# One power on GpSimd for the root, a VectorE-only residual update in a fixed order, and earlier places for the statistics' matmuls

## The chip, the cores and the metric

The kernel runs on one core of a Trainium2 chip. The metric is the device time of one execution in microseconds (us); lower is better. TensorE (PE) multiplies, VectorE (DVE) and GpSimd (POOL) do elementwise work, ScalarE (ACT) does activations and copies, and SyncE (SP) issues the loads.

## What is computed

A stack of eight sublayers works on 512 tokens of width 1024 in float32: two layers of a mixer with four gated branches and a SiLU feed-forward, then a recurrent block, an MLP, banded attention and another MLP. Around every sublayer stands an RMS norm; the four sublayers of the first block also norm their output before they add it to the residual:

```
def rmsnorm(x, g):
    y = xf * lax.rsqrt(jnp.mean(xf * xf, axis=-1, keepdims=True) + EPS)
    return (y * g.astype(jnp.float32)).astype(x.dtype)
...
    x = x + rmsnorm(merged @ w_out[l], g_post_mix[l])
    h = rmsnorm(x, g_pre_ffn[l])
    f = (jax.nn.silu(h @ w_ffn_gate[l]) * (h @ w_ffn_up[l])) @ w_ffn_down[l]
    x = x + rmsnorm(f, g_post_ffn[l])
```

## The kernel before, in words

Activations lie transposed: eight tiles of 128 features by 512 tokens. `self.x[k]` (tile name `xf`) is the residual. Each operand of a product is split into a high part and a low part (`xh`, `xl`; `wh`, `wl`), and `mm3` adds three matmuls: high by high, high by low, low by high. So a product needs the high part first (line 147) and the low part from its second or third matmul on (lines 148 and 149). The split of the residual for the next product (`norm_split`, by way of `split`) is an ACT copy with the gain as its scale (line 108) and a DVE subtraction (line 109).

The norm's factor never multiplies the operand: it is one number for each token and is applied to the result of the next product. It is made in four steps: squares are summed into `S` tile by tile (lines 215 to 219), `stats` lets PE sum them over the features (line 199, one column for each 128 tokens, result `ps_t`), `rsqrt` takes the root (lines 183 to 190: twelve small DVE instructions, a first guess from the bits and three Newton steps), and `spread` transposes the factor back over all partitions on PE (line 208). An ACT copy brings it to SBUF as `rb`.

`closing` ends the two mixers and the two feed-forwards (four times in all). It makes the last product of the sublayer in eight output tiles; the last four are made in two halves of 256 tokens, H0 and H1. After H0's four tiles come H0's statistics, root, transposes and `rb` while PE works on H1's tiles; `update` then multiplies each output tile by `rb` (line 248, DVE), adds it to the residual (line 249, POOL) and splits the new residual for the next sublayer's first product `self.first`, three output tiles at once, which begins with H0 as well. H1 gets the same one half later.

A scheduler sets the order of the instructions on each engine from data dependences and a timing model of its own. Inside `tc.issue_after(ins)` an instruction is placed after `ins`; `behind` in `gemm` uses this to hold the steps `k >= a` of a product back until the named instruction has its place in PE's queue. The lines that the change touches in `closing`:

```
behind = [(0, self.summed if j else None), (0, self.turned if j == 3 else None)] if cs is H1 else []
...
self.first = self.gemm(first, n.xs, gnext[2] if len(gnext) > 2 else "wide", halves=True,
                       behind=[(2, self.summed), (5, self.turned)])
```

`summed` is the last statistics matmul, `turned` the last transpose, `j` counts the four tiles made in halves.

Of the kernel before, what the change touches and what calls it, by code (L numbers as in the profile page):

```python
# [9 lines left out]
F32 = mybir.dt.float32  # L10
F32R = mybir.dt.float32r
I32 = mybir.dt.int32
AF = mybir.ActivationFunctionType
ALU = mybir.AluOpType
# [3 lines left out]
P = 128  # L18
# [3 lines left out]
EPS = 1e-6  # L22
# [4 lines left out]
ALL, H0, H1, ALLP = slice(0, 512), slice(0, 256), slice(256, 512), slice(0, P)  # L27
# [38 lines left out]
class Net:  # L66
    def __init__(self, ctx, tc, d, out):
        self.tc, self.nc, self.d, self.out = tc, tc.nc, d, out
        self.small = ctx.enter_context(tc.tile_pool(name="small", bufs=1))
        self.base = ctx.enter_context(tc.tile_pool(name="base", bufs=1))  # L70
        self.psum = ctx.enter_context(tc.tile_pool(name="psum", bufs=1, space=PSUM))
        self.prm = self.small.tile([P, NPRM], F32, name="prm")
        self.tab = self.small.tile([P, NTAB], F32, name="tab")
        self.uid = 0
        self.wide = 0
        self.after = []
# [99 lines left out]

    def rsqrt(self, y, src, n, scale):

        nc = self.nc
        v = self.t(self.small, "rs_v", 2, (P, 16))[:, :n]  # L180
        m = self.t(self.small, "rs_m", 2, (P, 16))[:, :n]
        w = self.t(self.small, "rs_w", 2, (P, 16))[:, :n]
        nc.vector.tensor_scalar(out=v, in0=src, scalar1=scale, scalar2=EPS, op0=ALU.mult, op1=ALU.add)
        nc.vector.tensor_scalar(out=m, in0=src, scalar1=-0.5 * scale, scalar2=-0.5 * EPS, op0=ALU.mult, op1=ALU.add)
        nc.vector.tensor_scalar(out=y.bitcast(I32), in0=v.bitcast(I32), scalar1=-0.5,
                                scalar2=float(0x5F3759DF), op0=ALU.mult, op1=ALU.add)
        for _ in range(3):
            nc.vector.tensor_tensor(out=w, in0=y, in1=y, op=ALU.mult)
            nc.vector.tensor_tensor(out=w, in0=w, in1=m, op=ALU.mult)
            self.rooted = nc.vector.scalar_tensor_tensor(out=y, in0=w, scalar=1.5, in1=y, op0=ALU.add, op1=ALU.mult)  # L190

    def stats(self, r, S, n, cs):

# [32 lines left out]
        n.rb = self.t(self.base, "rb", 2)  # L226
        return n

    def norm_split(self, n, k, cs):
        if n.xs[k] is None:  # L230
            n.xs[k] = self.pair(self.base, "x", KT)
        h, l = n.xs[k]
        x = self.x[k][:, cs]
        return self.split((h[:, cs], l[:, cs]), x, n.g[:, k:k + 1] if n.g is not None else None)

    def norm_step(self, n, k, cs):
        self.norm_split(n, k, cs)
# [4 lines left out]

    def update(self, fs, rb, n, cs):

        nc = self.nc
        for k in range(KT):
            f, x = fs[k][:, cs], self.x[k][:, cs]
            nc.vector.tensor_tensor(out=f, in0=f, in1=rb, op=ALU.mult)  # L248
            nc.gpsimd.tensor_tensor(out=x, in0=x, in1=f, op=ALU.add)
            last = self.norm_split(n, k, cs)  # L250
        return last


    def scores(self, it, qb):
# [91 lines left out]
    def mix(self, l, gnext):  # L346
        nc, tc, d = self.nc, self.tc, self.d
        V, S_, G = nc.vector, nc.scalar, nc.gpsimd
        N = self.norm
        xs, r, rb = N.xs, N.r, N.rb  # L350
# [6 lines left out]
        with tc.tile_pool(name=f"att{l}", bufs=1, reuse_waits="tile") as ap:  # L357
# [17 lines left out]
            for c in range(2):  # L375
                wh, wl = chunk(4 + c)
                for k in range(4):
                    x = xs[c * 4 + k]
# [6 lines left out]
            ps = self.ps("t")  # L385
# [29 lines left out]
            for i in range(4):  # L415
                f = vv[i // 2][:, i % 2 * 256:i % 2 * 256 + 256]
# [150 lines left out]
        with tc.tile_pool(name=f"gate{l}", bufs=1, reuse_waits="tile") as gp:  # L567
            self.wide = 0
            early = [self.gemm([chunk(16 + n)], xs)[0] for n in range(4)]
            br = {}  # L570
            for nm, fs in (("c", [outs["c0"], outs["c1"]]), ("b", [outs["b0"], outs["b1"]]),
                           ("d", [outs["d0"], outs["d1"]]), ("a", aout)):
                br[nm] = []
                for j, f in enumerate(fs):
                    if j % 2 == 0:
                        both = self.pair(gp, "wf", 5, (P, 2, T))
                    hl = (both[0][:, j % 2], both[1][:, j % 2])
                    self.split(hl, f)
                    br[nm].append(hl)
            ms = []  # L580
            for i in range(KT):
                m = self.t(gp, "m", 2)
                wo = None
                for n, nm in enumerate("cbda"):
                    ps = early.pop(0) if early else self.gemm([chunk(16 + i * 4 + n)], xs)[0]
                    g = self.t(gp, "g", 2)
                    V.tensor_tensor(out=g, in0=ps, in1=rb, op=ALU.mult)
                    S_.activation(out=g, in_=g, func=AF.Tanh, scale=0.5)
                    if nm == "a":
                        w = self.load(d["w_br"][l, i, :, 768:], 512)  # L590
                    else:
                        wo = wo or self.load(d["w_br"][l, i, :, :768], 768)
                        w = (wo[0][:, n * 256:n * 256 + 256], wo[1][:, n * 256:n * 256 + 256])
                    ps = self.gemm([w], br[nm])[0]
                    if n == 0:
                        V.scalar_tensor_tensor(out=m, in0=g, scalar=1.0, in1=ps, op0=ALU.add, op1=ALU.mult)
                    else:
                        V.scalar_tensor_tensor(out=g, in0=g, scalar=1.0, in1=ps, op0=ALU.add, op1=ALU.mult)  # L598
                        G.tensor_tensor(out=m, in0=m, in1=g, op=ALU.add)  # L599
                hl = self.pair(gp, "m_", 8)  # L600
                self.split(hl, m, scale=0.5)
                ms.append(hl)
            fs = [self.t(mp, tag, 4 if tag == "aout" else 1) for tag in ["aout"] * 4 + ["b0", "b1", "c0", "c1"]]

            def evac(S, i, ps, cs):
                S_.activation(out=fs[i][:, cs], in_=ps, func=AF.Copy, scale=self.c(f"g_post_mix{l}", i, i + 1))
                self.square_into(S[:, cs], ps, i == 0, V)

            self.closing(gp, 5, lambda i, **kw: self.load(d["w_out"][l, i], 1024, **kw), ms, evac, fs, gnext)
        keep.close()  # L610

    def closing(self, pool, nf, chunk, xs, evac, fs, gnext):


        nc, tc = self.nc, self.tc
        S = self.t(self.base, "S", 2)
        self.wide = 0
        for i in range(KT - 4):
            evac(S, i, self.gemm([chunk(i)], xs)[0], ALL)
        own = dict(pool=pool, tag="f", bufs=nf, raw=("raw", self.base))  # L620
        ws = [chunk(KT - 4, **own)] + [chunk(i) for i in range(KT - 3, KT)]
        first = [self.load(src, 1024, **own) for src in gnext[1][:3]]
        n = self.norm_begin(gnext[0])
        r = self.t(self.small, "r2", 2, (P, 4))
        for cs in (H0, H1):
            half = [(a[:, cs], b[:, cs]) for a, b in xs]
            for j, w in enumerate(ws):
                behind = [(0, self.summed if j else None), (0, self.turned if j == 3 else None)] if cs is H1 else []
                ps = self.gemm([w], half, pss=[self.ps("wide", (P, 256))], behind=behind)[0]
                evac(S, KT - 4 + j, ps, cs)  # L630
            nc.scalar.activation(out=n.rb[:, cs], in_=self.stats(r, S, D, cs), func=AF.Copy)
        for cs in (H0, H1):
            last = self.update(fs, n.rb[:, cs], n, cs)
        self.after = [last]
        self.ahead = [self.load(src, 1024) for src in gnext[1][3:]]
        self.first = self.gemm(first, n.xs, gnext[2] if len(gnext) > 2 else "wide", halves=True,
                               behind=[(2, self.summed), (5, self.turned)])
        for k in range(KT):
            self.square_into(n.S, self.x[k], k == 0, nc.vector)
        self.norm_end(n, ALL)  # L640
        self.after = [(self.rooted,)] * 9 + [last] * 2
        self.norm = n
# [523 lines left out]
```

## Time and profile before

| what | value |
|---|---|
| median of 3 runs | 2871.89 us (2869.84 to 2876.11) |
| profiled execution, its time | 2874.64 us |
| its span, first to last instruction | 2872.5 us |
| PE busy | 2769.2 us, 96% of the span |
| DVE busy | 1614.2 us, 56% |
| ACT busy | 1135.4 us, 40% |
| POOL busy | 520.6 us, 18% |
| mean granted PE clock | 0.979 |

The span is what the profile shows; 2.1 us of the execution lie outside it. PE's idle time is the difference between the span and its busy time, but a matmul at the lower of PE's two clock levels counts as busy too, so lost time hides in both. The four closings stand at about 445 to 488, 823 to 865, 1289 to 1331 and 1666 to 1709 us.

### The profile page before, as it was taken

The numbers are of one execution on the slowest core, as the hardware profiler recorded it, in microseconds if no ns is written. First come the engines' busy times: TensorE is split into PE (matmuls) and PEld (weight loads), VectorE is DVE, ScalarE is ACT, GpSimd is POOL, SyncE is SP. The second block draws the span as 40 slices with busy tenths as digits, with TensorE's granted clock in tenths as the row PEclk, the third lists the DMA queues.
The fourth block names the chain that finished last, engine by engine and source line by source line (L and its number), as shares of the span: only waits on it lengthen the run. The fifth ranks groups of instructions, "written<-read, shape, count | busy, mean of one in ns | idle before, by whom it ended". The sixth has DMA issues, their size and how long they took to land.

```text
span 2872.5 us, 34870 instructions
## 1 busy us (share of the span) xinstructions
PE 2769.2 (96%) x13616; PEld 2332.4 (81%) x13616; DVE 1614.2 (56%) x2615; ACT 1135.4 (40%) x1863; POOL 520.6 (18%) x419
## 2 busy tenths in 40 slices
PE   8999998999988999998999988899999999999999
PEld 7778888888887878887888876688888988788887
DVE  5874546534476765447344478844435677754443
ACT  4552334322243543233232346633223466643222
POOL 4301111100123211102000135400002553210000
PEclk9999999999999999999999989899999999999999
DMA  4212332323222113331323322133232222123222
GB/s 147 63 52 94 99 108 67 96 100 97 93 70 86 56 56 102 94 125 59 96 94 97 99 78 66 66 96 96 96 96 95 83 65 67 52 95 97 96 96 88
DMA packets 77061, 249.72 MB, mean 87 GB/s; under 512 B 8544, under 2 KB 14560, under 8 KB 76896
## 3 DMA queue, kind: packets, MB, share of 16 engines
q1 hardware_dynamic: 76896, 247.49, 26.8%
q8 instruction: 107, 1.75, 0.2%
q14 instruction: 58, 0.48, 0.1%
HBM read 245.36 MB, written 2.10 MB: 86 GB/s over the span
## 4 chain that ended last, share of the span: by engine, by line
PE 87%; DVE 9%; ACT 2%; issue 1%; POOL 0%; DMA 0%; ACTq 0%; DVEq 0%
PE ps_mm L148 16%; PE ps_mm L149 16%; PE ps_mm L147 16%; PE ps_s L147 9%; PE ps_s L148 8%; PE ps_s L149 8%; PE ps_o L148 3%; PE ps_o L149 3%; PE ps_o L147 3%; PE ps_o L304 1%; PE ps_t L293 1%; DVE f L248 1%; DVE y L730 1%; DVE p L281 1%; DVE xl L109 0%
## 5 line engine op out<-in xcount | busy, mean ns | idle before, releaser
L105 ACT ACTIVATE wh<-raw 128x1024 fp32r<-128x1024 f32 (+3 forms) x391 | 398.7, 1023 | 1180.5 <-PE ps_mm L148 444.5
L106 DVE TENSOR_TENSOR wl<-raw,wh 128x1024 fp32r<-128x1024 f32 (+3 forms) x391 | 497.3, 1274 | 152.3 <-ACT wh L105 144.0
L147 PE MATMUL ps_mm<-xh,wh 128*128 128x512 f32 x1176 | 462.8, 394 | 11.2 <-ACT xh L108 6.8
L148 PE MATMUL ps_mm<-xl,wh 128*128 128x512 f32 x1176 | 461.2, 392 | 0.5 <-DVE xl L109 0.5
L149 PE MATMUL ps_mm<-xh,wl 128*128 128x512 f32 x1176 | 460.6, 392 | 0.0
L147 PEld LDWEIGHTS ps_mm<-xh,wh 128*128 128x128 f32 x1176 | 222.8, 189 | 58.9 <-ACT xh L108 6.8
L148 PEld LDWEIGHTS ps_mm<-xl,wh 128*128 128x128 f32 x1176 | 222.7, 189 | 46.7 <-DVE xl L109 1.0
L149 PEld LDWEIGHTS ps_mm<-xh,wl 128*128 128x128 f32 x1176 | 222.4, 189 | 46.2
L147 PE MATMUL ps_s<-xh,wh 128*128 128x512 f32 x552 | 215.2, 390 | 0.0
L148 PE MATMUL ps_s<-xl,wh 128*128 128x512 f32 x552 | 214.8, 389 | 0.0
L149 PE MATMUL ps_s<-xh,wl 128*128 128x512 f32 x552 | 214.6, 389 | 0.0
L147 PE MATMUL ps_mm<-hh,wh 128*128 128x512 f32 (+1 forms) x438 | 167.4, 382 | 0.0
L149 PE MATMUL ps_mm<-hh,wl 128*128 128x512 f32 (+1 forms) x438 | 166.9, 382 | 0.0
L148 PE MATMUL ps_mm<-hl,wh 128*128 128x512 f32 (+1 forms) x438 | 166.9, 382 | 0.0
L665 POOL TENSOR_TENSOR a<-a,rb 128x512 f32<-128x512 f32 x44 | 60.8, 1384 | 567.0 <-DVE a L664 567.0
L140 POOL TENSOR_TENSOR wl<-raw,wh 128x1024 fp32r<-128x1024 f32 (+1 forms) x59 | 123.8, 2100 | 108.4 <-ACT wh L137 96.2
L599 POOL TENSOR_TENSOR m<-m,g 128x512 f32<-128x512 f32 x48 | 62.6, 1304 | 433.8 <-DVE g L598 433.7
L149 PEld LDWEIGHTS ps_s<-xh,wl 128*128 128x128 f32 x552 | 103.6, 188 | 21.9 <-DVE wl L106 0.3
L147 PEld LDWEIGHTS ps_s<-xh,wh 128*128 128x128 f32 x552 | 103.7, 188 | 21.4
L148 PEld LDWEIGHTS ps_s<-xl,wh 128*128 128x128 f32 x552 | 103.6, 188 | 21.3
L147 PE MATMUL ps_s<-hh,wh 128*128 128x512 f32 (+1 forms) x300 | 113.9, 380 | 0.0
L148 PE MATMUL ps_s<-hl,wh 128*128 128x512 f32 (+1 forms) x300 | 113.7, 379 | 0.0
(476 smaller groups left out, 6010.3 us busy)
## 6 DMA issues: line engine op xcount, KB each, us to landing
raw<-in_w_in SPq DMA_DIRECT2D x96, 512.0 KB, 3.5
raw<-in_w_gu SPq DMA_DIRECT2D x88, 512.0 KB, 3.5
raw<-in_w_down SPq DMA_DIRECT2D x80, 512.0 KB, 3.5
raw<-in_w_up SPq DMA_DIRECT2D x64, 512.0 KB, 3.5
raw<-in_w_down SPq DMA_DIRECT2D x32, 448.0 KB, 3.3
raw<-in_w_qkv SPq DMA_DIRECT2D x24, 512.0 KB, 3.4
raw<-in_w_out SPq DMA_DIRECT2D x16, 512.0 KB, 3.5
raw<-in_a_w_in SPq DMA_DIRECT2D x16, 512.0 KB, 3.4
```

What stands on the lines that cost most here:

```text
L105: a = nc.scalar.activation(out=h, in_=src, func=AF.Copy)
L106: b = (eng or nc.vector).tensor_tensor(out=l, in0=src, in1=h.bitcast(F32), op=ALU.subtract)
L140: eng.tensor_tensor(out=l[:, a:b], in0=raw[:, a:b], in1=h[:, a:b].bitcast(F32), op=ALU.subtract)
L147: mm(out=ps, lhsT=a[0], rhs=b[0], start=first, stop=False)
L148: mm(out=ps, lhsT=a[0], rhs=b[1], start=False, stop=False)
L149: mm(out=ps, lhsT=a[1], rhs=b[0], start=False, stop=last)
L248: nc.vector.tensor_tensor(out=f, in0=f, in1=rb, op=ALU.mult)
L281: nc.vector.tensor_scalar(out=p[:, :w], in0=p[:, :w], scalar1=sm, scalar2=None, op0=ALU.mult)
L293: self.mark = nc.tensor.transpose(out=pt[:, ks], in_=p[:, ks], identity=self.c("ident"))
L304: nc.tensor.matmul(out=o[:, kb * P:], lhsT=it["v"](kb), rhs=pt[:, bs], start=kb == 0 and pt is pth, stop=kb == 3 and pt is ptl)
L599: G.tensor_tensor(out=m, in0=m, in1=g, op=ALU.add)
L665: G.tensor_tensor(out=a, in0=a, in1=rb, op=ALU.mult)
```

## The change

Three edits. The root is two instructions: a DVE scale-and-offset (`rs_v`), and one POOL power with exponent -0.5 from a constant tile `half`. This holds for every use of `rsqrt`: the norms, two small norms in each mixer, and eight calls of 16 columns in attention. In `update` the residual add goes from POOL to DVE, and all DVE instructions are chained in one order: multiply and add of tile k, then the low part of tile k-1. The matmuls for the statistics go into PE's queue ahead of step 6 of the first H1 tile (before: behind that whole tile), the transposes ahead of step 3 of the second H1 tile (before: anywhere ahead of the last tile), and in the next product ahead of step 4 (before: step 5). In the mixers the square now comes ahead of the scaled copy on ACT.

```
 def rsqrt(self, y, src, n, scale):
     v = self.t(self.small, "rs_v", 2, (P, 16))[:, :n]
-    nc.vector.tensor_scalar(out=v, in0=src, scalar1=scale, scalar2=EPS, op0=ALU.mult, op1=ALU.add)
-    nc.vector.tensor_scalar(out=m, in0=src, scalar1=-0.5 * scale, scalar2=-0.5 * EPS, op0=ALU.mult, op1=ALU.add)
-    nc.vector.tensor_scalar(out=y.bitcast(I32), in0=v.bitcast(I32), scalar1=-0.5,
-                            scalar2=float(0x5F3759DF), op0=ALU.mult, op1=ALU.add)
-    for _ in range(3):
-        nc.vector.tensor_tensor(out=w, in0=y, in1=y, op=ALU.mult)
-        nc.vector.tensor_tensor(out=w, in0=w, in1=m, op=ALU.mult)
-        self.rooted = nc.vector.scalar_tensor_tensor(out=y, in0=w, scalar=1.5, in1=y, op0=ALU.add, op1=ALU.mult)
+    self.rooted = self.nc.vector.tensor_scalar(out=v, in0=src, scalar1=scale, scalar2=EPS, op0=ALU.mult, op1=ALU.add)
+    self.nc.gpsimd.tensor_tensor(out=y, in0=v, in1=self.half[:, :n], op=ALU.pow)
...
+    def norm_parts(self, n, k, cs):
+        (h, l), x, g = self.norm_pair(n, k, cs)
+        return (lambda: self.nc.scalar.activation(out=h, in_=x, func=AF.Copy, scale=g),
+                lambda: self.nc.vector.scalar_tensor_tensor(out=l, in0=x, scalar=g, in1=h.bitcast(F32), op0=ALU.mult,
+                                                            op1=ALU.subtract))
...
 def update(self, fs, rb, n, cs):
-    nc = self.nc
+    V = self.nc.vector
+    last = rest = None
+    def chain(make):
+        nonlocal last
+        with self.tc.issue_after(last.ins) if last is not None else ExitStack():
+            last = make()
     for k in range(KT):
         f, x = fs[k][:, cs], self.x[k][:, cs]
-        nc.vector.tensor_tensor(out=f, in0=f, in1=rb, op=ALU.mult)
-        nc.gpsimd.tensor_tensor(out=x, in0=x, in1=f, op=ALU.add)
-        last = self.norm_split(n, k, cs)
-    return last
+        chain(lambda: V.tensor_tensor(out=f, in0=f, in1=rb, op=ALU.mult))
+        chain(lambda: V.tensor_tensor(out=x, in0=x, in1=f, op=ALU.add))
+        if rest:
+            chain(rest)
+        head, rest = self.norm_parts(n, k, cs)
+        head = head()
+    chain(rest)
+    return head, last
...
-                behind = [(0, self.summed if j else None), (0, self.turned if j == 3 else None)] if cs is H1 else []
+                behind = [(0 if j else 6, self.summed), ((99, 3, 0, 0)[j], self.turned)] if cs is H1 else []
...
-                               behind=[(2, self.summed), (5, self.turned)])
+                               behind=[(2, self.summed), (4, self.turned)])
```

The first place is DVE's queue where H0's update starts in the first mixer's closing. `aout`, `b` and `c` are output tiles, `xl` the low parts that the next product needs, `S` with `sq` the running sum of squares. Before:

```order
L219 TENSOR_TENSOR S_3534<-S_3534,sq_3912 128x256
L248 TENSOR_TENSOR aout_3526<-aout_3526,rb_3717 128x256
L248 TENSOR_TENSOR aout_3527<-aout_3527,rb_3717 128x256
L248 TENSOR_TENSOR aout_3528<-aout_3528,rb_3717 128x256
L248 TENSOR_TENSOR aout_3529<-aout_3529,rb_3717 128x256
L248 TENSOR_TENSOR b_744_3530<-b_744_3530,rb_3717 128x256
L248 TENSOR_TENSOR b_745_3531<-b_745_3531,rb_3717 128x256
L248 TENSOR_TENSOR c_746_3532<-c_746_3532,rb_3717 128x256
L248 TENSOR_TENSOR c_747_3533<-c_747_3533,rb_3717 128x256
L219 TENSOR_TENSOR S_3534<-S_3534,sq_3941 128x256
L109 SCALAR_TENSOR_TENSOR xl_3998<-xf_66,prm,xh_3997 128x256
```

The same place with the change (lines 259 and 260 multiply and add, 236 makes the low part, 213 sums squares):

```order
L213 TENSOR_TENSOR S_3500<-S_3500,sq_3836 128x256
L259 TENSOR_TENSOR aout_3492<-aout_3492,rb_3683 128x256
L260 TENSOR_TENSOR xf_68<-xf_68,aout_3492 128x256
L259 TENSOR_TENSOR aout_3493<-aout_3493,rb_3683 128x256
L260 TENSOR_TENSOR xf_69<-xf_69,aout_3493 128x256
L236 SCALAR_TENSOR_TENSOR xl_3940<-xf_68,prm,xh_3939 128x256
L259 TENSOR_TENSOR aout_3494<-aout_3494,rb_3683 128x256
L213 TENSOR_TENSOR S_3500<-S_3500,sq_3865 128x256
L260 TENSOR_TENSOR xf_70<-xf_70,aout_3494 128x256
L236 SCALAR_TENSOR_TENSOR xl_3946<-xf_69,prm,xh_3945 128x256
```

The first low part stood behind eight multiplies and a sum of squares, and now stands behind two multiplies and two adds.

The second place is PE's queue around H0's statistics (line 199, now 193) and transposes (line 208, now 202) in the same closing; `ps_mm` and `ps_s` are the first and second H1 tile. Before, the statistics stand behind the whole first tile, and the transposes 45 rows later, in the third tile:

```order
L148 MATMUL ps_mm_3857<-m_l_3523,wfh_3674 128x256
L149 MATMUL ps_mm_3857<-m_h_3522,wfl_3675 128x256
L199 MATMUL ps_t_3835<-prm,S_3534 128x1 x2
L147 MATMUL ps_s_3886<-m_h_2164,wh_3680 128x256
...
L148 MATMUL ps_s_3915<-m_l_3329,wh_3686 128x256
L208 MATMUL ps_t_3853<-tab,r_792_3718 128x128 x2
L149 MATMUL ps_s_3915<-m_h_3328,wl_3687 128x256
```

With the change:

```order
L152 MATMUL ps_mm_3811<-m_h_3100,wfl_3641 128x256
L193 MATMUL ps_t_3801<-prm,S_3500 128x1 x2
L150 MATMUL ps_mm_3811<-m_h_3294,wfh_3640 128x256
...
L152 MATMUL ps_s_3840<-m_h_2324,wl_3647 128x256
...
L152 MATMUL ps_s_3840<-m_h_2518,wl_3647 128x256
L202 MATMUL ps_t_3807<-tab,r_786_3684 128x128 x2
L150 MATMUL ps_s_3840<-m_h_2712,wh_3646 128x256
```

The statistics moved up by six matmuls, and the transposes now follow them after 15 matmuls instead of 44. In the feed-forwards, whose products have seven steps, 12 matmuls stand between them now, and in H1's turn, inside the next product, 18 in all four closings (27 before).

The third place is POOL's queue in the first mixer's closing, from the last gate product on. Where 16 residual adds stood there are three powers:

```order
L614 TENSOR_TENSOR m_3298<-m_3298,g_3464 128x512
L184 TENSOR_TENSOR r_786_3684<-rs_v_3804,half 128x2
L184 TENSOR_TENSOR r_786_3684<-rs_v_3930,half 128x2
L184 TENSOR_TENSOR r_3682<-rs_v_4197,half 128x4
L680 TENSOR_TENSOR a_4219<-a_4219,rb_3683 128x512
```

Nothing else is left on POOL between the gates and the feed-forward.

## Rows read from the trace of the kernel before

**Rows 1.** The page: busy time of each engine; the chain that ended last, by engine.

```profile
PE 2769.2 (96%) x13616; PEld 2332.4 (81%) x13616; DVE 1614.2 (56%) x2615; ACT 1135.4 (40%) x1863; POOL 520.6 (18%) x419
...
PE 87%; DVE 9%; ACT 2%; issue 1%; POOL 0%; DMA 0%; ACTq 0%; DVEq 0%
```

**Rows 2.** Waits of PE, whole span: us in total, times, longest.

```profile
PE ps_mm L148 <- DVE xl L109: 34.0, 9, 4.7
...
PE ps_t L208 <- DVE r L190: 4.4, 1, 4.4
...
PE ps_mm L147 <- DVE tt L366: 3.3, 1, 3.3
```

**Rows 3.** Windows, the four closings: length, busy PE, PEld, DVE, ACT, POOL, clock, DMA.

```profile
445.48:488.37 42.89, 34.60 (x256) 34.10 (x255) 32.38 (x70) 18.99 (x39) 13.90 (x16) 0.88 0.05 14
823.13:864.61 41.48, 33.05 (x238) 32.55 (x237) 34.31 (x77) 19.54 (x39) 13.85 (x16) 0.88 0.06 17
1288.51:1331.43 42.92, 34.64 (x257) 34.14 (x255) 32.39 (x70) 19.01 (x39) 13.88 (x16) 0.88 0.05 18
1666.18:1708.72 42.54, 34.11 (x244) 33.53 (x243) 35.16 (x75) 20.60 (x40) 17.61 (x18) 0.84 0.06 18
```

**Rows 4.** Timeline of PE, first closing: start, us, instruction [idle before, releaser].

```profile
448.92 0.28 PE L148 MATMUL ps_s<-m_l,wh 128*128 128x256 f32 x1
...
454.07 0.38 PE L208 MATMUL ps_t<-tab,r 128*128 128x128 f32 x2
...
457.66 0.52 PE L147 MATMUL ps_mm<-xh,wfh 128*128 128x256 f32 x3
462.69 0.58 PE L148 MATMUL ps_mm<-xl,wfh 128*128 128x256 f32 x1 [4.52 <-DVE xl L109]
463.07 0.42 PE L149 MATMUL ps_mm<-xh,wfl 128*128 128x256 f32 x1
...
473.93 0.52 PE L147 MATMUL ps_mm<-xh,wfh 128*128 128x256 f32 x3
478.23 0.58 PE L148 MATMUL ps_mm<-xl,wfh 128*128 128x256 f32 x1 [3.78 <-DVE xl L109]
```

**Rows 5.** Timeline of DVE, first closing.

```profile
448.90 0.16 DVE L183 TENSOR_SCALAR rs_v<-ps_t 128x2 f32<-128x2 f32 x1 [2.02 <-PE ps_t L199]
448.98 0.15 DVE L184 TENSOR_SCALAR rs_m<-ps_t 128x2 f32<-128x2 f32 x1
...
451.07 0.16 DVE L190 SCALAR_TENSOR_TENSOR r<-rs_w,r 128x2 f32<-128x2 f32 x1
...
454.91 2.53 DVE L248 TENSOR_TENSOR aout<-aout,rb 128x256 f32<-128x256 f32 x4 [1.82 <-ACT rb L631]
...
461.70 1.34 DVE L109 SCALAR_TENSOR_TENSOR xl<-xf,prm,xh 128x256 fp32r<-128x256 f32 x2
```

**Rows 6.** Four lines' instructions: duration in ns, shortest, median and longest.

```profile
L248 DVE TENSOR_TENSOR f<-f,rb x32: 412/942/968, 832.0 to 1695.4; 128x256 f32<-128x256 f32 x32
...
L249 POOL TENSOR_TENSOR xf<-xf,f x32: 837/903/920, 832.5 to 1696.9; 128x256 f32<-128x256 f32 x32
...
L109 DVE SCALAR_TENSOR_TENSOR xl<-xf,prm,xh x88: 468/476/1784, 7.3 to 2526.2; 128x256 fp32r<-128x256 f32 x64, 128x512 fp32r<-128x512 f32 x24
...
L219 DVE TENSOR_TENSOR S<-S,sq x72: 412/679/2721, 425.3 to 1707.6; 128x512 f32<-128x512 f32 x40, 128x256 f32<-128x256 f32 x32
```

**Rows 7.** POOL: a small instruction in the timeline; the longest group by form.

```profile
4.83 0.20 POOL L706 TENSOR_TENSOR sc<-sc 128x8 f32<-128x8 f32 x1
...
L140 POOL TENSOR_TENSOR wl<-raw,wh 128x1024 fp32r<-128x1024 f32 x32 | 82.1, 2566 | 93.6 <-ACT wh L137 81.5 <-ACT wqh L105 9.7 <-PE ps_s L147 2.2
```

**Rows 8.** Timeline of DVE, POOL and PE behind the fourth closing.

```profile
1714.92 2.29 DVE L185 TENSOR_SCALAR r<-rs_v 128x4 int32<-128x4 int32 x1
...
1714.84 2.34 POOL L140 TENSOR_TENSOR wl<-raw,wh 128x1024 fp32r<-128x1024 f32 x1 [3.20 <-ACT wh L137]
...
1719.12 1.08 PE L208 MATMUL ps_t<-tab,r 128*128 128x128 f32 x4 [4.44 <-DVE r L190]
```

More of the change, by code (lines that the diff above doesn't have):

```diff
@@ L72, in __init__ @@
         self.prm = self.small.tile([P, NPRM], F32, name="prm")
+        self.half = self.small.tile([P, 64], F32, name="half")
+        self.nc.gpsimd.memset(self.half[:, :16], -0.5)
         self.tab = self.small.tile([P, NTAB], F32, name="tab")
@@ L177, in rsqrt @@
     def rsqrt(self, y, src, n, scale):
-        nc = self.nc
         v = self.t(self.small, "rs_v", 2, (P, 16))[:, :n]
-        m = self.t(self.small, "rs_m", 2, (P, 16))[:, :n]
-        w = self.t(self.small, "rs_w", 2, (P, 16))[:, :n]
-        nc.vector.tensor_scalar(out=v, in0=src, scalar1=scale, scalar2=EPS, op0=ALU.mult, op1=ALU.add)
-        nc.vector.tensor_scalar(out=m, in0=src, scalar1=-0.5 * scale, scalar2=-0.5 * EPS, op0=ALU.mult, op1=ALU.add)
-        nc.vector.tensor_scalar(out=y.bitcast(I32), in0=v.bitcast(I32), scalar1=-0.5,
-                                scalar2=float(0x5F3759DF), op0=ALU.mult, op1=ALU.add)
-        for _ in range(3):
-            nc.vector.tensor_tensor(out=w, in0=y, in1=y, op=ALU.mult)
-            nc.vector.tensor_tensor(out=w, in0=w, in1=m, op=ALU.mult)
-            self.rooted = nc.vector.scalar_tensor_tensor(out=y, in0=w, scalar=1.5, in1=y, op0=ALU.add, op1=ALU.mult)
+        self.rooted = self.nc.vector.tensor_scalar(out=v, in0=src, scalar1=scale, scalar2=EPS, op0=ALU.mult, op1=ALU.add)
+        self.nc.gpsimd.tensor_tensor(out=y, in0=v, in1=self.half[:, :n], op=ALU.pow)
     def stats(self, r, S, n, cs):
@@ L227, in norm_begin, with norm_pair @@
         return n
-    def norm_split(self, n, k, cs):
+    def norm_pair(self, n, k, cs):
         if n.xs[k] is None:
@@ L232, in norm_split @@
         h, l = n.xs[k]
-        x = self.x[k][:, cs]
-        return self.split((h[:, cs], l[:, cs]), x, n.g[:, k:k + 1] if n.g is not None else None)
+        return (h[:, cs], l[:, cs]), self.x[k][:, cs], n.g[:, k:k + 1] if n.g is not None else None
+    def norm_split(self, n, k, cs):
+        return self.split(*self.norm_pair(n, k, cs))
+    def norm_parts(self, n, k, cs):
[3 more added lines that the diff above has]
+                                                            op1=ALU.subtract))
     def norm_step(self, n, k, cs):
@@ L243, in update @@
     def update(self, fs, rb, n, cs):
-        nc = self.nc
+        V = self.nc.vector
[4 more added lines that the diff above has]
+                last = make()
         for k in range(KT):
             f, x = fs[k][:, cs], self.x[k][:, cs]
-            nc.vector.tensor_tensor(out=f, in0=f, in1=rb, op=ALU.mult)
-            nc.gpsimd.tensor_tensor(out=x, in0=x, in1=f, op=ALU.add)
-            last = self.norm_split(n, k, cs)
-        return last
+            chain(lambda: V.tensor_tensor(out=f, in0=f, in1=rb, op=ALU.mult))
[6 more added lines that the diff above has]
+        return head, last
     def scores(self, it, qb):
@@ L605, in evac @@
             def evac(S, i, ps, cs):
+                self.square_into(S[:, cs], ps, i == 0, V)
                 S_.activation(out=fs[i][:, cs], in_=ps, func=AF.Copy, scale=self.c(f"g_post_mix{l}", i, i + 1))
-                self.square_into(S[:, cs], ps, i == 0, V)
             self.closing(gp, 5, lambda i, **kw: self.load(d["w_out"][l, i], 1024, **kw), ms, evac, fs, gnext)
```

## The prediction

> **What bounds the kernel now.** I read the page first. PE is busy for 96% of the span and the chain that ended last is 87% PE [rows 1], so time can be won only where PE waits, or where it works at the lower of its two clock levels. Next the waits of PE: the largest by far is for `xl`, the low part of the residual, 34.0 us in nine waits; one for the root (4.4 us) and one for a mixer's first scaled product (3.3 us) also touch the change [rows 2]. Then the windows of the four closings, from the first H1 tile to the end of the next sublayer's first product [rows 3]. Together they last 169.8 us, and PE is busy for 136.4, so it idles 33.4. The reader is to see that this is nearly the whole 34.0 us, and that the clock in them is 0.84 to 0.88 instead of 1.
>
> What should these stretches take? A matmul of 256 columns passes in 0.12 us: 71 of them and the transposes lie between 448.92 and 457.66 [rows 4]. A mixer's closing has 4x24 of them and then 2x72, a feed-forward's (seven steps) 4x21 and 2x72, so 936 in all, 112.3 us. Eight sets of statistics (about 0.36 each) and transposes (about 0.2) make 4.5, some 8 matmuls of 512 columns 2. That is 119 us, against 136.4 busy: 17.5 us are the lower clock, which sets in behind the waits (at 463.07, right behind one, a matmul lasts 0.42 us, at 448.92 0.28, [rows 4]). Idle and clock together, 51 us are lost, 12.7 a closing.
>
> Why does PE wait? In the first closing the factor is multiplied in from 454.91, but the first `xl` starts at 461.70 [rows 5], because eight multiplies stand ahead of it. PE began the next product at 457.66 and stood until 462.69; for H1 the same from 473.93 to 478.23 [rows 4].
>
> **The change part by part.** *The fixed order.* Multiply and add hardly get cheaper. A DVE multiply takes 0.41 us undisturbed, but its median is 0.94 beside a POOL add of 0.90 [rows 6]: they take turns, so a tile costs about 0.9 us for both. On DVE alone a multiply and the add that needs it take about 0.46 + 0.34 = 0.80 (0.42 each, 0.04 for the dependence, 0.08 overlap as `rs_v` and `rs_m` show, [rows 5]). That is 0.1 us a tile, 0.8 a half. The Trainium skill (GPSIMD Engine Reference, 3.1 Elementwise) says that a GpSimd add of two tensors takes 1.96 times VectorE's. By that ratio alone one would book 0.45 us a tile, 29 us over 64 tiles; the rows say that most of this is not there, since the multiply was being stretched by the same add. What counts is the place of the first `xl`: behind four instructions instead of nine. That is 4 x 0.4 + 0.47 = 2.0 us behind `rb`, where it was 461.70 - 454.91 = 6.8 to its start. Even with `rb` at 454.91 it would end at 456.9, before PE asks for it.
>
> *Root and queue places.* In the first closing, step 6 of the first H1 tile is at 445.48 + 18 x 0.12 = 447.6, the statistics end at 448.0, and `rs_v` starts 0.2 later, with the second matmul behind them (448.90 and 448.92, [rows 4, 5]). With 0.16 for it, two hand-overs of 0.1 and a power of p, the root is there at 448.6 + p. The Newton chain took 448.90 to 451.23. PE reaches the transposes after 15 matmuls, at 449.8; so p up to 1.2 us costs nothing. In the feed-forwards, with 12 matmuls, the limit is 0.85, in H1's turn (18) 1.55. The trace has no power. From below stands a POOL multiply of 8 columns at 0.20, from above POOL's longest group, 1024 columns, at 2.57 [rows 7]. With 2 columns it is nearer to the first, but a power is more than a multiply: I take 1.0, an estimate (0.15 us too long in the feed-forwards' H0). Then `rb` follows 0.84 behind the transposes (454.07 to 454.91, [rows 4, 5]): the multiply starts at 450.7, not 454.9, and the first `xl` ends at 452.7, 5 us before PE needs it.
>
> *What is late next.* DVE now needs 0.80 + 0.39 = 1.19 us a tile, and 1.79 where the square sum of the next norm stands between (0.68 less the overlap, [rows 6]); PE eats a tile in 9 x 0.12 = 1.08. In H0 the lead of 5 us holds. In H1 the transposes are at 457.66 + 4 x 1.08 + 0.36 = 462.3, the multiply at 463.2, `xl` of tile 0 at 465.2, of tile 1 at 466.4, then one each 1.79: tile 6 at 475.4. PE starts H1 at 466.9 and wants tile 6 at 473.6. So some 1.8 us of waiting stays, with 0.4 for the clock: 2.2 a closing. The gain is 51 - 4 x 2.2 = 42 us.
>
> *Behind the fourth closing* PE waits 4.44 us for the root because one small DVE instruction took 2.29 us, just while POOL ran a split of 2.34 [rows 8]. Now one DVE instruction and a power stand there. The power is ahead of that split in POOL's queue, so the split waits for it instead. With p = 1, about 1.5 us of the wait stays: gain 3. The second mixer's 3.3 us [rows 2] hangs on a root as well; I book 1 (bounds 0 and 3.3).
>
> *At nothing*: the square ahead of the copy on ACT (idle 56% of each closing, [rows 3]); the constant tile, made at the start; the other roots, whose transposes stand 20 or more matmuls behind, and attention's eight of 16 columns, which can wait behind a POOL split of up to 2.57 us, as small DVE instructions do now (bounds: 8 x 2.3 gained, as much lost). DMA volume and buffers stay; the scheduler reshuffles the mixers' openings and attention, for which I allow 6 us either way.
>
> **Sum.** 42 + 3 + 1 = 46. The profiled execution took 2874.64 (span 2872.5 and 2.1 around it), so 2828.6 on its own basis; it lies 2.7 us above the median of 2871.89, so 2826 against that. Of the reshuffling I put 2 us on the losing side: 2828.
>
> **The rivals.** *A dearer power*, 2 to 4 us. At p = 3 PE waits for the root 1.8 or 2.15 us in H0 and 1.45 in H1, and each wait costs some clock too: 5 us a closing and 3 elsewhere, so 2851. For it: nothing in the trace bounds it below 2.57; against it: it works on 2 to 4 columns.
>
> *Reshuffling or a slower DVE chain.* If each dependent add costs 0.2 us more, DVE needs 1.4 us a tile, the H0 lead goes, and the statistics of H1, which wait for the last square sum in that same queue, come late: 3 us a closing, 12 in all, or as much lost in attention or the mixers' openings: 2840 to 2855.
>
> *The power eats it all* (slower). The place is the transposes in PE's queue, where everything behind waits in order. The price in a closing is (p - 1.2) + (p - 1.55), with 3 us for the clock, against 10.6 gained: it turns at p = 5.2. At p = 8 the closings lose 20 us and the other roots as much again: about 2910. For it: the root now stands close behind the statistics, with 12 to 18 matmuls of cover instead of 27 to 44. Against it: no POOL instruction in the page takes that long by group mean, at up to 1024 columns.
>
> *No effect.* The waits could move to `xh` on ACT: about 0.5 us each, one per tile, beside DVE's two instructions. That would leave 2866 to 2877; little speaks for it.
>
> **How the numbers follow.** The case of the sum 0.63 (own range 2814 to 2838), dearer power 0.15, reshuffling or slow chain 0.11, no effect 0.03, power eats it 0.08. The range goes from 2812 to 2860, which leaves out the slower cases and the dearest powers. Faster by over 0.2% (about 6 us, what a measurement of this kernel can tell from no change): 0.63 + 0.15 + 0.11 = 0.89; same 0.03; slower 0.08.
>
> **What would show it.** Right: the first `xl` starts about 2 us behind the first multiply, the power is near 1 us, PE has no wait over 2 us in the four stretches, they shrink from 42.5 to about 32 us each, and their clock is above 0.95. Wrong: a wait of PE for `r` at the transposes of 2 us or more in each half (dear power), waits for `xl` that grow from tile to tile in H0 (DVE too slow), or new waits in attention and the mixers' openings. A power of over 5 us would turn the sign.

## The result, and the profile after

The changed kernel takes 2823.08 us (median of 4 runs, 2821.85 to 2823.62), the kernel before 2870.86 us on the same chip (4 runs, 2867.89 to 2876.11): a ratio of 0.9826, 95% interval 0.9813 to 0.9839. Forecast were 2828 us and faster. The profiled execution took 2822.87 us with a span of 2821.1, so between the profiled executions, which the sums below go by, the gain is 51.8 us; between the medians it is 47.8.

First the page of the changed kernel, busy time by engine and the chain that ended last:

```profile
PE 2753.3 (98%) x13616; PEld 2315.4 (82%) x13616; DVE 1565.7 (56%) x2371; ACT 1137.2 (40%) x1863; POOL 505.3 (18%) x384
...
PE 86%; DVE 9%; POOL 2%; ACT 1%; DMA 1%; issue 1%; POOLq 0%; DVEq 0%; ACTq 0%
```

PE's busy time fell by 16 us [rows 1] with the same 13616 matmuls. In the four closings alone it fell by 16.3, from 136.4 [rows 3] to 120.1, while the granted clock there rose to 1.00 from 0.84 in one and 0.88 in three; the rest of the gain is idle time. The waits of PE (line 151 is the old 148, line 236 the low part in the update, line 202 the transposes):

```profile
PE ps_mm L150 <- ACT xh L111: 6.8, 1, 6.8
PE ps_s L150 <- ACT U L111: 5.8, 2, 4.3
PE ps_mm L150 <- DVE y L778: 5.0, 1, 5.0
...
PE ps_mm L151 <- DVE xl L236: 2.7, 8, 0.3
```

The wait for `xl` went from 34.0 us to 2.7 [rows 2] and is no longer at the head of the list. The three at its head are for operands that the change does not make; those for `U` and `y` were 3.6 and 3.2 us before and stand in the recurrent block, where other waits became shorter. The windows of the four closings, with their sum:

```profile
445.46:476.80 31.34, 30.68 (x255) 30.27 (x254) 24.77 (x62) 17.70 (x38) 1.51 (x2) 1.00 0.01 1
812.12:842.15 30.03, 29.36 (x242) 28.87 (x240) 26.22 (x67) 18.20 (x38) 1.56 (x2) 1.00 0.01 4
1258.63:1289.96 31.33, 30.67 (x254) 30.26 (x253) 24.76 (x62) 17.68 (x38) 1.51 (x2) 1.00 0.01 1
1625.29:1655.31 30.02, 29.36 (x243) 28.90 (x241) 26.21 (x67) 18.18 (x38) 1.57 (x3) 1.00 0.01 4
sum 122.72, PE 120.07 PEld 118.30 DVE 101.97 ACT 71.75 POOL 6.16; mean PE 30.02 PEld 29.57 DVE 25.49 ACT 17.94 POOL 1.54
```

They were 169.8 us [rows 3]: 47.1 are gained, PE idles 0.66 or 0.67 in each, and the clock is 1.00 throughout. PE's busy time in them is 120.1 us, where 119 were worked out as the least. The same in the timeline of the first closing, rows of PE and then rows of DVE with POOL's power:

```profile
447.62 0.50 PE L193 MATMUL ps_t<-prm,S 128*128 128x1 f32 x4
...
449.85 0.38 PE L202 MATMUL ps_t<-tab,r 128*128 128x128 f32 x2
...
473.23 0.39 PE L151 MATMUL ps_mm<-xl,wfh 128*128 128x256 f32 x1 [0.34 <-DVE xl L236]
...
474.90 0.39 PE L151 MATMUL ps_mm<-xl,wfh 128*128 128x256 f32 x1 [0.33 <-DVE xl L236]
```

```profile
448.16 0.16 DVE L183 TENSOR_SCALAR rs_v<-ps_t 128x2 f32<-128x2 f32 x1 [1.66 <-PE ps_t L193]
448.40 0.71 POOL L184 TENSOR_TENSOR r<-rs_v,half 128x2 f32<-128x2 f32 x1 [33.82 <-DVE rs_v L183]
...
450.69 0.43 DVE L259 TENSOR_TENSOR aout<-aout,rb 128x256 f32<-128x256 f32 x1 [0.87 <-ACT rb L646]
...
452.29 0.48 DVE L236 SCALAR_TENSOR_TENSOR xl<-xf,prm,xh 128x256 fp32r<-128x256 f32 x1
...
466.02 0.48 DVE L236 SCALAR_TENSOR_TENSOR xl<-xf,prm,xh 128x256 fp32r<-128x256 f32 x1
...
467.69 0.48 DVE L236 SCALAR_TENSOR_TENSOR xl<-xf,prm,xh 128x256 fp32r<-128x256 f32 x1
```

The power takes 0.71 us. PE passes the transposes without a stop, and the multiply starts at 450.69 (454.91 before, [rows 5]). The first `xl` ends at 452.77, and PE takes it up at 457.76, five microseconds later. In H1 one `xl` comes every 1.67 us. Durations by line, over the whole span:

```profile
L259 DVE TENSOR_TENSOR f<-f,rb x32: 416/420/428, 817.0 to 1651.6; 128x256 f32<-128x256 f32 x32
...
L260 DVE TENSOR_TENSOR xf<-xf,f x32: 414/424/427, 817.5 to 1652.5; 128x256 f32<-128x256 f32 x32
...
L184 POOL TENSOR_TENSOR r<-rs_v,half x18: 695/1006/2074, 27.9 to 2480.2; 128x4 f32<-128x4 f32 x8, 128x2 f32<-128x2 f32 x8, 128x8 f32<-128x8 f32 x2
L184 POOL TENSOR_TENSOR fac<-rs_v,half x8: 2897/2926/3928, 2187.9 to 2375.8; 128x16 f32<-128x16 f32 x8
```

Without POOL beside it the multiply needs 0.42 us, where its median was 0.94 [rows 6]. The power's price follows its columns: 0.70 at two, 1.0 at four, 2.1 at eight, 2.9 at sixteen. Behind the fourth closing:

```profile
1660.28 2.36 POOL L143 TENSOR_TENSOR wl<-raw,wh 128x1024 fp32r<-128x1024 f32 x1 [1.71 <-ACT wh L140]
...
1661.74 0.16 DVE L183 TENSOR_SCALAR rs_v<-ps_t 128x4 f32<-128x4 f32 x1 [2.09 <-PE ps_t L193]
...
1662.60 1.01 POOL L184 TENSOR_TENSOR r<-rs_v,half 128x4 f32<-128x4 f32 x1
...
1663.66 0.65 PE L202 MATMUL ps_t<-tab,r 128*128 128x128 f32 x4 [1.68 <-POOL r L184]
```

The wait fell from 4.44 [rows 8] to 1.68 us. The power starts 0.70 us behind `rs_v`, where it was 0.08 in the first closing, since it stands behind a split that POOL had already begun.

Where the time went, by stretches between fixed points of PE's program (us; attention runs from the statistics ahead of it to those behind it):

| stretch | before | after |
|---|---|---|
| four closings | 169.8 | 122.7 |
| closing 2 to closing 3 (second mixer's opening and products) | 423.9 | 416.5 |
| closing 4 to the recurrent block's end | 176.4 | 172.0 |
| attention | 292.9 | 298.8 |
| closing 1 to 2, closing 3 to 4, first MLP | 1021.9 | 1023.5 |

Gained are 47.1 + 7.4 + 4.5, lost 6.0 in attention and 1.6 in the last line: 51.4, the difference of the spans.

### The profile page after: what moved, and what is told of

Its sections match the earlier page's. It is cut to its first block, busy times and chain, and to the rows that moved or that the text cites. A ratio compares the mean times of both kernels' runs of the same rounds, so it can differ in the third digit from the quotient of the medians.

```text
span 2821.1 us, 34584 instructions
## 1 busy us (share of the span) xinstructions
PE 2753.3 (98%) x13616; PEld 2315.4 (82%) x13616; DVE 1565.7 (56%) x2371; ACT 1137.2 (40%) x1863; POOL 505.3 (18%) x384
## 4 chain that ended last, share of the span: by engine, by line
PE 86%; DVE 9%; POOL 2%; ACT 1%; DMA 1%; issue 1%; POOLq 0%; DVEq 0%; ACTq 0%
PE ps_mm L151 15%; PE ps_mm L150 15%; PE ps_mm L152 15%; PE ps_s L150 9%; PE ps_s L151 9%; PE ps_s L152 9%; PE ps_o L151 3%; PE ps_o L152 3%; PE ps_o L150 3%; PE ps_o L319 1%; PE ps_t L308 1%; DVE y L745 1%; DMA raw<-in_w_qkv 1%; DVE xl L236 1%; DVE S L213 0%
```

## The experiments

Theory: the closings waited for the first low part, which stood behind eight multiplies, and for a late factor; the order of the update carries most of the gain, root and places the rest. Rival: the length of the root is what counted. To be explained besides: attention's loss of 6 us. The runs were timed in several rounds, in which the kernel before had medians of 2870.9 to 2874.1 us; each ratio is to the kernel before of the same round, and the stretches are those of each run's one profiled execution.

| run | median, us | four closings | closing 2 to 3 | closing 4 on | attention |
|---|---|---|---|---|---|
| changed kernel | 2823.1 | 122.7 | 416.5 | 172.0 | 298.8 |
| order alone | 2845.4 | 139.3 | 425.1 | 174.5 | 291.0 |
| power alone | 2861.9 | 163.3 | 420.9 | 172.7 | 292.8 |
| old root in the changed kernel | 2839.5 | 134.4 | 423.2 | 173.9 | 294.9 |
| add on GpSimd | 2832.5 | 132.3 | 416.2 | 172.3 | 297.3 |
| old root at 16 columns only | 2815.5 | 122.7 | 415.6 | 173.7 | 291.3 |
| root 4 powers long | 2835.5 | 134.3 | 420.0 | 177.1 | 292.0 |
| root 11 powers long | 2936.7 | 184.0 | 428.8 | 185.4 | 305.8 |

**Order alone.** The kernel before with the new `update`, which also moves the add to VectorE:

```
...
-            nc.gpsimd.tensor_tensor(out=x, in0=x, in1=f, op=ALU.add)
-            last = self.norm_split(n, k, cs)
+            chain(lambda: V.tensor_tensor(out=x, in0=x, in1=f, op=ALU.add))
+            if rest:
+                chain(rest)
...
```

> The kernel before with the fixed VectorE order of the update alone (residual add on VectorE); old root, old places in PE's queue. Theory: the place of the first low part carries most of the gain. In H0 it ends about 2 us behind the factor, at 457, before PE asks; in H1 a wait of 2 to 3 us is left because the factor is later there: 36 to 40 of the 47 us in the closings are gained, nothing elsewhere: 2830 to 2838. Rival: root and places carry half or more of it: 2845 to 2860.

2845.36 us (ratio 0.9903, 0.9889 to 0.9916). The time misses the theory's range and lies at the lower edge of the rival's, 2845 to 2860; the stretches tell more. The closings gain 30.5 of the 47.1 us, 6 to 10 less than expected, but well over half. These 30.5 hold the order and the add's move together: no run has the new order in the kernel before with the add on GpSimd, and none has the new places with the old order. The wait for `xl` is gone (1.6 us), and PE now waits for the root, 2.5 to 2.6 us in H1 of every closing. The sum of the four windows, and the wait in the whole span (its fifth is outside the closings):

```profile
sum 139.31, PE 127.36 PEld 124.31 DVE 111.52 ACT 73.08 POOL 0.02; mean PE 31.84 PEld 31.08 DVE 27.88 ACT 18.27 POOL 0.00
...
PE ps_t L208 <- DVE r L190: 12.8, 5, 2.6
```

The timeline of DVE in the first closing of this run shows why:

```profile
462.43 0.16 DVE L183 TENSOR_SCALAR rs_v<-ps_t 128x2 f32<-128x2 f32 x1 [0.23 <-PE ps_t L199]
462.51 0.15 DVE L184 TENSOR_SCALAR rs_m<-ps_t 128x2 f32<-128x2 f32 x1
462.57 0.42 DVE L266 TENSOR_TENSOR xf<-xf,b 128x256 f32<-128x256 f32 x1
462.90 0.16 DVE L185 TENSOR_SCALAR r<-rs_v 128x2 int32<-128x2 int32 x1
462.97 0.48 DVE L242 SCALAR_TENSOR_TENSOR xl<-xf,prm,xh 128x256 fp32r<-128x256 f32 x1
...
467.94 0.16 DVE L190 SCALAR_TENSOR_TENSOR r<-rs_w,r 128x2 f32<-128x2 f32 x1
```

H1's root starts while H0's update still runs, and its twelve small instructions stand between wide ones in the same queue: from 462.43 to 468.10, 5.7 us, where H0's took 2.33, as long as before [rows 5].

**Power alone.** The kernel before with the new `rsqrt` only:

```
...
-        for _ in range(3):
...
+        self.nc.gpsimd.tensor_tensor(out=y, in0=v, in1=self.half[:, :n], op=ALU.pow)
```

> The kernel before with the power alone: every root is one power, the update keeps its old order with the add on GpSimd, the statistics and transposes their old places. In a closing the root comes about 1.1 us earlier in each half, while the first low part still stands behind eight multiplies. Theory: the closings gain no more than that, 1 to 3 us each with the clock, 4 to 12 in all; the second mixer's opening gives its 7 us and the place behind the fourth closing 2 to 4; attention loses about 6 if its last quarter falls to the lower clock again, so 2852 to 2866. Rival (the power is the main part of the gain): 2845 or less. Second rival (alone it brings nothing, since the queue holds the transposes anyway): 2868 or more.

2861.91 us (ratio 0.9956, 0.9939 to 0.9972), as the theory had it: the closings gain 6.5 us, PE still waits 25.3 us for `xl` in nine waits. The second mixer gave 3.0 us where 7 were expected. Attention does not lose, though all its powers are there.

**Old root in the changed kernel.** The twelve VectorE instructions back in `rsqrt`, order and places kept.

> The changed kernel with the old root of twelve VectorE instructions everywhere; fixed order and new places in the queue stay. From the first small instruction to the root it takes 2.3 us, where scale-and-offset, hand-overs and power take about 1.1. Theory: the power is the smaller part. PE waits 0.8 us in a mixer's H0, 1.2 in a feed-forward's, 0.5 in H1, with clock about 2 us a closing, 8 in all; behind the fourth closing and in the second mixer's opening 4 to 10 us come back; attention gets its 6 back: 2829 to 2836. Rival: the length of the root is what the closings waited for: 5 us or more a closing come back, 2845 or more.

2839.49 us (ratio 0.9881, 0.9865 to 0.9896), between the theory's range and the rival's. The sum of the four windows, and the wait in the whole span:

```profile
sum 134.40, PE 121.44 PEld 118.26 DVE 113.11 ACT 72.05 POOL 0.01; mean PE 30.36 PEld 29.57 DVE 28.28 ACT 18.01 POOL 0.00
...
PE ps_t L211 <- DVE r L193: 12.9, 9, 2.6
```

The closings lose 11.7 us, 10.3 of them in waits for the root at the transposes: 0.71 and 0.87 us in a mixer, 1.50 and 2.07 in a feed-forward, with the clock still at 1.00. Against order alone the places, with the earlier square in the mixers, are worth 4.9 us; once they are there the power is worth 11.7, where alone it gave 6.5. Attention got back 3.9 of the 6 us that were expected.

**The add on GpSimd.**

```
-            chain(lambda: V.tensor_tensor(out=x, in0=x, in1=f, op=ALU.add))
+            self.nc.gpsimd.tensor_tensor(out=x, in0=x, in1=f, op=ALU.add)
```

> The changed kernel with the residual add back on GpSimd; VectorE's order (multiply of a tile, then the low part of the tile before it), the power and the places stay. Theory: the place counts and the engine hardly. Multiply and add take turns at about 0.9 us a tile, the first low part is about 1 us later, which H0's lead covers; in H1 the slower rate costs 1 to 3 us a closing: 2827 to 2835. Rival by the ratio of 1.96 alone: 0.45 us a tile on the path, 29 us: about 2850. Second rival: no difference at all, 2820 to 2826.

2832.45 us (ratio 0.9856, 0.9841 to 0.9870): 9.4 more than the changed kernel by the medians, within the theory's range. In the profiled execution, the fastest of the four at 2827.62 us, the closings take 9.6 us more and the rest 4.9 less. Durations of the add on POOL here:

```profile
L260 POOL TENSOR_TENSOR xf<-xf,f x32: 731/852/1122, 816.0 to 1658.1; 128x256 f32<-128x256 f32 x32
```

That is 2.01 times the 424 ns on DVE. The Trainium skill (GPSIMD Engine Reference, 3.1 Elementwise) gives 1.96 for this ratio, and the rows agree. The difference of 0.43 us over 64 tiles would be 27 us, and a third of it is found. In H1 of the first closing one `xl` comes every 1.81 us in this run, where it is 1.67 with the add on VectorE: 0.14 us a tile and not 0.43. The add runs while VectorE makes the square sum and the low part, and the low part beside it takes 0.95 us instead of 0.48.

**The old root at 16 columns only.** Attention's eight roots with the twelve instructions, the power everywhere else:

```
+        if n < 16:
+            self.nc.gpsimd.tensor_tensor(out=y, in0=v, in1=self.half[:, :n], op=ALU.pow)
+            return
```

> The changed kernel, but attention's eight roots of 16 columns are again the twelve VectorE instructions. Theory: attention's loss of 6 us (292.9 us before, 298.8 with the change) comes from the power of 16 columns, which takes 2.9 us on GpSimd and stands there among splits of 2.4 us, so that the scaled q and k come late: attention falls back to 292 to 294 us and the whole to about 2817. Rival: the loss is a chance of the order the scheduler makes, or of the clock in attention's last quarter, and not of the power: attention stays at 297 to 301 us, the whole at 2821 to 2826.

2815.51 us (5 runs, 2814.52 to 2817.62; ratio 0.9799, 0.9785 to 0.9812). Attention falls to 291.3 us, and this is the fastest version that keeps the computation. It looked like the theory's proof; the next runs say that it is not.

**Two columns of sixteen; and every such power twice.** The first leaves the factor wrong in the other 14 columns, so it leaves out a part of attention's computation.

```
+        if n == 16:
+            self.nc.vector.tensor_scalar(out=y[:, 2:], in0=v[:, 2:], scalar1=0.1, scalar2=None, op0=ALU.mult)
+            y, v, n = y[:, :2], v[:, :2], 2
```

> The changed kernel, but of attention's 16-column roots only two columns go through the power; the other 14 columns of the factor are a VectorE copy times 0.1, so q and k are scaled by wrong numbers there (that part of the computation is left out). The instruction on GpSimd stays at its place in the chain, at 0.7 instead of 2.9 us. Theory (the 2.2 us on GpSimd cost attention its time): attention at 291 to 294 us, the whole at 2814 to 2818. Rival (the change of the scheduler's order does it, whatever the instruction costs): attention at 297 us or more, the whole at 2821 or more.

2814.14 us (ratio 0.9793, 0.9778 to 0.9807), attention 291.3.

```
+        if n == 16:
+            w = self.t(self.small, "rs_w", 2, (P, 16))
+            self.nc.gpsimd.tensor_tensor(out=w, in0=v, in1=self.half[:, :n], op=ALU.pow)
```

> The changed kernel with every 16-column power of attention made twice, one behind the other on GpSimd, so the factor comes 2.9 us later. Theory (time on GpSimd in the chain to q and k): attention grows by another 3 to 8 us to 302 to 307, the whole to 2826 to 2832. Rival (order of the instructions and where the clock happens to fall): no growth by rule, attention anywhere between 291 and 300.

2822.42 us (ratio 0.9820, 0.9803 to 0.9836), attention 299.1. The first agrees with the theory, the second does not: the power that counts comes second in the trace, so every factor is 2.9 us later, and attention grows by 0.3.

**The power several times, first attempt.** Three or ten more powers ahead of the one that counts, for roots of up to four columns (the edit with three):

```
+        if n <= 4:
+            w = self.t(self.small, "rs_w", 2, (P, 16))[:, :n]
+            for _ in range(3):
+                self.nc.gpsimd.tensor_tensor(out=w, in0=v, in1=self.half[:, :n], op=ALU.pow)
```

> The changed kernel with every power of up to four columns made four times in a row on GpSimd (the first three into a scratch tile): p goes from 0.7 to about 2.8 us at two columns and from 1.0 to 4.0 at four. The prediction's price for p = 3: PE waits 1.8 or 2.2 us at H0's transposes and 1.5 at H1's, 5 us a closing with the clock, and 3 to 8 us at the roots of four columns: 2845 to 2851. Rival: a cover the prediction did not see, closings unchanged, below 2830. Second rival: longer waits take the clock down for whole products, 8 us or more a closing, 2860 or more.

> The same with eleven powers in a row: p is about 7.7 us at two columns, 11 at four. The prediction's rule: a closing costs (p - 1.2) + (p - 1.55) + 3 us of clock = 16 us against the changed kernel, 64 in the four, and with the roots of four columns 75 to 90 in all: 2895 to 2915, slower than the kernel before, whose level is passed at p = 5.2. Rival: the other work in a closing (low parts that H0's lead and the deeper queue cover) takes up a part, so that a closing loses 10 us or less and the whole stays under 2875.

2827.87 us (2823.58 to 2832.01; ratio 0.9840, 0.9824 to 0.9856) and 2825.63 us (ratio 0.9832, 0.9817 to 0.9847). Neither tests what it should: the scheduler put the power that counts in second place, so p was 1.4 in both. For that value the runs are good: a mixer's closing does not wait, a feed-forward's waits 0.16 us in H0. And attention, with its eight powers of 2.9 us untouched, is at 291.8 and 291.5 us.

**The power several times, in order.** The same, with each power placed after the one before it and the root last.

> The changed kernel with every root of up to four columns made by four powers in a row, in a fixed order, and only the last of them gives the root: p is about 2.8 us at two columns and 4 at four. (In the runs before, the scheduler put the power that counts in second place, so that p was only 1.4.) The prediction's price for p = 3 is 5 us a closing and 3 elsewhere. Attention's bare stretch is 138 matmuls here, so about 7 us come back there: 2837 to 2842. Second reading, from the run with the old root (whose waits of 0.7 to 2.1 us cost 2 us a mixer's closing and 3.9 a feed-forward's): about 3 us a closing, 2828 to 2836. Rival: no loss in the closings at all, 2816 to 2820.

> The same with eleven powers in a row, the last of them the root: p is about 7.7 us at two columns and 11 at four. The prediction's rule gives 16 us a closing against the changed kernel, and as much as 10 to 25 at the other roots, with about 7 back in attention: 2888 to 2905, slower than the kernel before; the level of before is passed at p = 5.2. Rival: the queues take up part of it, 10 us or less a closing, and the whole stays under 2870.

2835.47 us (ratio 0.9873, 0.9857 to 0.9890) and 2936.73 us (ratio 1.0225, 1.0207 to 1.0243). Rows of PE in the first closing, with four powers (p = 2.72) and then with eleven (7.37):

```profile
449.16 0.43 PE L206 MATMUL ps_t<-tab,r 128*128 128x128 f32 x2 [1.15 <-POOL r L188]
...
462.78 0.43 PE L206 MATMUL ps_t<-tab,r 128*128 128x128 f32 x2 [0.88 <-POOL r L188]
```

```profile
470.16 0.69 PE L206 MATMUL ps_t<-tab,r 128*128 128x128 f32 x2 [5.81 <-POOL r L188]
...
490.53 0.69 PE L206 MATMUL ps_t<-tab,r 128*128 128x128 f32 x2 [5.60 <-POOL r L188]
```

With four powers the closings lose 11.6 us, 2.9 each, and the clock in them stays at 1.00. With eleven they lose 61.2, 15.3 each, at a clock of 0.85; by the medians everything else loses 52 more, so the whole went beyond the expected 2905.

**Attention's filler spread.** One number in the changed kernel:

```
-                self.heads(items, filler(), 20 if qt == 3 else 99, 1000, 2)
+                self.heads(items, filler(), 8 if qt == 3 else 99, 1000, 2)
```

> The changed kernel with one number changed in attention's last quarter: the product steps that fill the gaps between the heads are tied to the heads' transposes from the 8th step on instead of the 20th. All powers stay, attention's eight of 2.9 us too. In the program's order for PE the longest stretch of attention's last quarter with no product in it is 116 matmuls, against 150 in the three runs with attention at 297 to 299 us, and 117 to 138 in those at 291 to 295. Theory (the new order made that bare stretch longer, PE's clock goes to the lower level in it, and the power's duration has nothing to do with it): attention 290 to 293 us, the whole 2814 to 2818. Rival (the power's 2.9 us in the chain to q and k): attention stays at 297 to 300, the whole at 2821 to 2825.

2832.09 us (ratio 0.9858, 0.9842 to 0.9873), above both ranges: attention took 308.8 us, ten more. The count of matmuls without a product was no measure. What does go with attention's time is the clock. The window of 40 us that starts 200 us into attention, of the changed kernel, of the old root at 16 columns, and of this run (clock is the third number from the end; 1.00 is the upper of its two levels throughout, 0.50 the lower throughout):

```profile
2380.15:2420.15 40.00, 37.28 (x150) 27.86 (x149) 28.07 (x89) 27.60 (x71) 10.51 (x14) 0.70 0.08 27
```

```profile
2380.98:2420.98 40.00, 36.06 (x181) 26.29 (x181) 31.87 (x103) 29.59 (x74) 11.06 (x13) 0.96 0.10 33
```

```profile
2381.25:2421.25 40.00, 37.88 (x121) 28.22 (x121) 24.85 (x79) 24.59 (x61) 11.29 (x13) 0.50 0.06 21
```

PE passes 150, 181 and 121 matmuls in the same time, and its idle time does not differ so much (2.7, 3.9 and 2.1 us). In other runs the window reads 0.66 with every power twice, 0.91 before and with power alone, 0.96 with eleven powers unordered and with four in order; attention takes 299.1, 292.9, 292.8, 291.5 and 292.0 us there. With the old root everywhere, where attention has no power at all, it reads 0.75 and attention takes 294.9 us: the clock falls there without the power too.

## Why the forecast held, step by step

*Where the loss was*: right. Of the 51.4 us between the spans 47.1 come out of the four windows.

*The fixed order*: right in mechanism. The first `xl` starts 1.60 us behind the first multiply, as the count of four instructions gave (2.0 to its end, measured 2.08). Alone, with the add's move, it yields 30.5 us. The ratio of the engines was rightly not booked: on GpSimd the add costs 9.4 us, not 29.

*Root and places*: right. p is 0.71 to 0.81 in the closings where 1.0 was taken, the multiply starts at 450.69 where 450.7 was forecast, and no transposes wait. The limit in a feed-forward's H0 is about 1.24 (0.16 us of wait at p = 1.4), not 0.85. What the text missed is why the power helps most once the order is fixed: the old root is not a chain of 2.3 us there, since it shares a queue with the update (2.5 to 3.9 us in the closings of the changed kernel with the old root).

*What is late next*: right in place, mis-sized. "One each 1.79" measured 1.67, and of "some 1.8 us of waiting", "with 0.4 for the clock", 0.67 and no clock were left. The gain in the closings was therefore 47.1 and not 42.

*Behind the fourth closing*: the wait became 2.8 us shorter, where 3 were booked, and the stretch as a whole 4.5. The sentence that the power is ahead of that split in POOL's queue was wrong for the split that counted: it was running already.

*The second mixer*: mis-sized, 7.4 where 1 was booked (bounds 0 and 3.3). The bound was the wait alone; the clock behind it is missing from it. The first 58 us behind the second closing, before, in the changed kernel, and with the old root in it (PE's matmuls are in the first bracket, the clock is third from the end):

```profile
864.98:923.00 58.02, 54.05 (x308) 47.05 (x307) 34.79 (x84) 22.72 (x47) 21.67 (x14) 0.94 0.26 84
```

```profile
842.03:900.00 57.97, 56.91 (x343) 50.10 (x342) 38.02 (x67) 27.69 (x56) 29.67 (x20) 1.00 0.32 101
```

```profile
846.65:905.00 58.35, 56.57 (x336) 49.14 (x335) 45.47 (x99) 26.37 (x55) 23.46 (x16) 1.00 0.31 101
```

Most of the gain is made here, and the old root keeps most of it: its chain takes 2.1 us there, where it took 4.2 before with one small instruction of 2.26. That the whole stretch is nevertheless back at 423.2 with the old root comes mainly from the next 50 us, where the clock is 0.90, against 0.97 in the changed kernel, and PE waits 3.5 us for `p`, against 1.3. So it is not shown that the shorter root is the cause of the 7.4.

*The reshuffling*: 2 us were put on the losing side, attention alone lost 6.0, at the edge of the 6 allowed. This error and that of the second mixer nearly cancel, and that is luck: the sum of 46 stood against 51.4 between the spans.

*The rivals.* The dearer power's rule, (p - 1.2) + (p - 1.55) with clock, gives 15.0 us at p = 7.37 with 3 us of clock, and 15.3 were measured; at 2.72 the waits alone, 2.7, are the measured 2.9, and the clock added to make 5 was not lost. The sign turns between: on the line through the two runs' medians at p = 4.35, where 5.2 was forecast, because what lies outside the closings cost 52 us at p = 7.37, where 20 were put for p = 8. The closings by themselves, on the line through the same two runs, are back at their 169.8 us of before only at p = 6.0 or so. The slower DVE chain did not come: dependent adds follow within 0.46 us. The rival's other half, a loss in attention, did come: attention's lower clock goes with the 7.6 us by which the kernel lies above its best version. That the scheduler's new order causes it is not shown.

*Open*: why the clock falls in attention's last quarter in some programs and not in others. The power's duration is not it (2.9 us more in every factor cost 0.3, and four programs with the same powers run at 291.5 to 292.8), nor the number of matmuls without a product. The run with three extra powers, timed at 2823.6, 2824.3, 2831.5 and 2832.0 us with mean granted clocks of 0.991, 0.990, 0.987 and 0.987, hints that one program can go both ways, but only one execution has a profile.

## What to carry to other kernels

Before an instruction is made faster, look what stands ahead of it in its own queue: putting the first consumer's input behind four instructions instead of nine was worth more than either the faster root (6.5 us alone, 11.7 last) or the freed engine (9.6). The run with the new order gave 30.5 with the add's move in it; less those 9.6, an estimate from two different kernels, the order is left with about 21. A chain of many small instructions costs its own length only while nothing else is queued on that engine (2.33 us here, 5.7 between wide ones); replaced by one instruction on an idle engine it gave 11.7 us here, once the queue had become full. Prove a gain in a remote stretch by perturbing it more than once, since here a single run pointed to the wrong cause.

## What the runs showed of the hardware that was not expected

A power on GpSimd of 128 partitions costs 0.70 us at two columns and 2.9 at sixteen, 0.10 to 0.27 us for each further column. At eight it is 2.07, ten times the 0.20 of a multiply of eight [rows 7].

In the closings with the new order, waits of PE of up to 2.1 us left the granted clock at 1.00; with one wait of 2.5 to 2.6 us a closing (order alone) it was 0.95, with two of 5.6 to 6.2 us (eleven powers) 0.85. A price for the clock on every wait, as the forecast had it, was too much for these short ones. But the length of a wait does not settle it. With the power alone PE waits the same 1.76 and 3.78 us in the first closing and in the third, and behind the 1.76 the clock went to its lower level in the first and not in the third:

```profile
446.72:489.09 42.37, 36.68 (x256) 35.77 (x255) 30.18 (x49) 18.92 (x39) 15.51 (x18) 0.84 0.07 23
...
1284.68:1324.95 40.27, 34.09 (x256) 33.27 (x255) 30.26 (x49) 18.91 (x39) 15.52 (x18) 0.92 0.08 27
```
